# Twenty of the 120 taps of a depthwise convolution move from the vector engine to the scalar engine and accumulating DMAs

## The chip, the cores and the metric

The kernel runs on one core of one Trainium2 chip. The metric is the device time of one execution in microseconds (us), the median of several runs. Beside it stands a profiled execution of the same program; every time of a single instruction comes from that one.

## What is computed

Two transformer-like blocks in sequence on one sequence of 512 tokens and 1024 features, all in float32. The first block mixes tokens by pooling and gating, attends to a memory of 256 entries, and ends in a feed-forward part with a three-tap convolution. The second block is the one that matters here:

```
h = rms_norm(x, norm1_g)
q, k, v, glu_a, glu_b = split(h @ w_in)
q, k = rms_norm(q per head, q_norm_g), rms_norm(k per head, k_norm_g)
attn = stick_breaking_attention(q, k, v)              # 8 heads of 64, causal

c = glu_a * sigmoid(glu_b)                            # 512 tokens x 512 channels
c = causal_depthwise_conv(c, conv_dw_w, conv_dw_b)    # 31 taps
c = silu(layer_norm(c, conv_ln_g, conv_ln_b))

x = x + concat(attn, c) @ w_out
x = x + conv_ffn(rms_norm(x, norm2_g))
```

The depthwise convolution has 31 taps. For each of four chunks of 128 channels (channels lie on the partitions, the 512 tokens along the free dimension) it is 31 products of a shifted 128x512 tile with one weight per channel, added up.

## The kernel before, in words

**Products.** Float32 matrix products are done as three matmuls on operands that are split into a high and a low part (`mm3`, lines 126 to 129). Weights are loaded 1024 KB at a time into `raw` by SyncE's DMA queue, and `prep` (line 178) makes the two parts: ScalarE casts the high one (L199), and VectorE subtracts to get the low one (L205). For eight weight units of this stage (`SUMMED`, line 63) the low part is made in another way: ScalarE writes the negated weights (L202), and a DMA from GpSimd's queue adds `raw` onto that (L203, `accum_op`).

**The stage around the change.** After the first block's feed-forward part TensorE computes, in this order: the gated unit's chunks 0 and 1 (`glu`, line 697), the queries (`heads("G", ...)`), chunk 2, the keys (`heads("F", ...)`), chunk 3, the values (`project`, lines 960 to 969), and then the attention in twelve blocks (`sticks`, `breaks`, `gather`). While TensorE works on this, VectorE does the convolution's taps one at a time as filler (`conv`, L851): one instruction multiplies a shifted 128x512 view of `cc` (the slot H0) by a column of weights and adds it onto `cv` (the slot H1). One tap of each chunk is done by ScalarE, which starts the sum with the bias (L848 by way of L132). `TURNS` lists the chunk of each of the other 120 taps, and each call of `conv(n, after)` releases the next n of them, behind a given instruction.

**Heads.** For each of four tiles of 128 tokens, `heads` (line 728) multiplies into a bank of PSUM, ScalarE squares the tile (L742), VectorE sums over each head (L744), GpSimd makes the inverse root in three small instructions (L745, L746, L747: multiply and add, power, multiply), and VectorE scales the tile into `norm2` (L748, the slot D1). When all four tiles are there TensorE transposes them (L755), eight 128x128 pieces for the first two tiles and eight for the other two, and ScalarE and VectorE split the result (L143, L144) into the queries or keys that the attention reads.

**The norm.** `conv_norm` (line 884) normalizes the convolution's result over the channels. It is written behind the attention: four matmuls with ones give the mean (L889), VectorE subtracts it (L893), ScalarE squares (L895), VectorE adds up (L897), four small matmuls and a power on GpSimd give the inverse root (L902, L906, L334), one matmul spreads it (L911), VectorE scales (L915), and ScalarE applies SiLU (L917).

**Order.** The order on each engine is not the order in which the code is written. A list scheduler places each instruction at build time by its own estimate of when it can start, so a change of one part moves others; every engine then runs its list strictly in that order. Where an instruction waits, all those behind it on its engine wait too.

Of the kernel before, what the change touches and what calls it, by code (L numbers as in the profile page):

```python
# [10 lines left out]
F32 = mybir.dt.float32  # L11
F32R = mybir.dt.float32r
I32 = mybir.dt.int32
AF = mybir.ActivationFunctionType
# [65 lines left out]
def block_kernel(  # L80
# [91 lines left out]
    def half(name, a, b, dt=F32R):  # L172
        return part(slot(name, dt), a, b)
# [523 lines left out]
    def glu(i):  # L697
        pt = sta_unit(ph, pl)
        if i == 0:
            norms()  # L700
        ab = v3(t4(), 2, 512)
        dve.tensor_tensor(ab, pt, over2(rb2), ALU.mult)
        sig = act.activation(ab[:, 1, :], ab[:, 1, :], AF.Sigmoid)
        if i == 3:
            with tc.issue_after(sig.ins):
                act.preload_act_table_set(tables)
        return dve.tensor_tensor(cc[:, i, 30:542], ab[:, 0, :], ab[:, 1, :], ALU.mult)  # L707
# [67 lines left out]
    def sticks(hp, n):  # L775

        w = WIDE[n]
        zt = pair()
        z = zt[:, :, :w]

        for i, (ks, qs) in enumerate(((kT[0], qT[0]), (kT[0], qT[1]), (kT[1], qT[0]))):
            for a in STEPS[n]:
                for e in range(2):
                    hs = slice(e * HD, (e + 1) * HD)
                    pe.matmul(z[:, e, cols_of(a)], ks[hs, hp, a * P : (a + 1) * P],  # L785
                              qs[hs, hp, a * P :], start=i == 0 and a < 3, stop=False,
                              skip_group_check=True)
        for a in STEPS[n]:
            for e in range(2):
                pe.matmul(z[:, e, cols_of(a)][:, :P], identr, never, start=False, stop=False,  # L790
                          skip_group_check=True)
        ex = v3(t4(), 2, w)
        if hp < 2:
            act.activation(ex, z, AF.Abs)
        else:

            dve.tensor_scalar(ex.bitcast(I32), z.bitcast(I32), 0x7FFFFFFF, None,
                              ALU.bitwise_and)
        act.activation(ex, ex, AF.Exp, scale=-1.0)
        act.activation(ex, ex, AF.Ln, bias=1.0)  # L800
        dve.scalar_tensor_tensor(ex, z, 0.0, ex, ALU.max, ALU.add)
        zs[hp, n] = z
        return copy_split(*blk(hp, n), ex)
# [28 lines left out]

    TURNS = [0] * 8 + [0, 1] * 22 + [1, 2] * 8 + [2, 3] * 22 + [3] * 8
    done = [0] * 4
    tap = None

    def conv(n, after=None):

        nonlocal tap
        tap = after or tap
        for _ in range(min(n, len(TURNS))):
            i = TURNS.pop(0)
            k = done[i]
            done[i] += 1
            if k == 0:
                identity(cv[:, i, :], cc[:, i, 30:542], scale=par("dw_w", 4 * 30 + i),  # L848
                         bias=par("dw_b", i))
            with tc.issue_after(tap.ins) if tap else nullcontext():  # L850
                tap = dve.scalar_tensor_tensor(  # L851
                    cv[:, i, :], cc[:, i, k : k + 512], par("dw_w", 4 * k + i), cv[:, i, :],
                    ALU.mult, ALU.add)
# [2 lines left out]
    conv(8, glu(0))  # L856
    split_early(2)
    conv(16, glu(1))
    qT = heads("G", "qg", HD ** -0.5, (0, 4, 4, 8), lambda: conv(8, glu(2)), early[:2])
    kT = heads("F", "kg", 1.0, (0, 6, 5, 8), lambda: conv(12, glu(3)), early[2:])  # L860
    v2 = half("E0", 4, T, F32)
    stk = {}

    def place(i):
# [106 lines left out]
    seq = [(hp, n) for hp in range(4) for n in range(3)]  # L971

    conv(10, sticks(*seq[0]))
    conv(14, sticks(*seq[1]))
    project()
    todo = 2
    for i, x in enumerate(seq):
# [138 lines left out]
```

## Time and profile before

| | |
|---|---|
| median of 3 runs | 1245.53 us (1244.4 to 1246.41) |
| the profiled execution | 1245.94 us, its span 1244.2 us |
| TensorE busy | 1230.3 us, 99% of the span |
| VectorE busy | 754.0 us, 61% |
| ScalarE busy | 495.0 us, 40% |
| GpSimd busy | 113.5 us, 9% |

The span is the time from the first to the last instruction on the core; the rest of the 1245.94 us lies around it. PE is TensorE's matmul row, PEld its weight load, DVE VectorE, ACT ScalarE, POOL GpSimd and SP SyncE. A DMA that an engine starts is listed with that engine; the time "to landing" runs from the start of the issuing instruction to the arrival of its data.

### The profile page before, as it was taken

Reading aid. Unit: us, or ns where it says so; the run is one execution under the profiler, and the core shown is the slowest. Engines: PE = TensorE matmul, PEld = TensorE weight load, DVE = VectorE, ACT = ScalarE, POOL = GpSimd, SP = SyncE. Lnnn points to the kernel's source line nnn. Section 1 sums busy time; section 2 is a strip of 40 time slices with the busy share of each in tenths; the row PEclk is TensorE's granted clock in tenths of the full one; section 3 lists DMA queues with packets and bytes.
Section 4 is the critical chain, followed back from the end, with each engine's and each line's share of the span. In section 5 each row is a group of like instructions: output and inputs, shape, how many; then the busy total and the mean of one; then the engine's idle time right before and its main releaser. Section 6 shows DMA issues by size and latency. Waiting matters only on the chain.

```text
span 1244.2 us, 13667 instructions
## 1 busy us (share of the span) xinstructions
PE 1230.3 (99%) x5712; PEld 1014.1 (82%) x5712; DVE 754.0 (61%) x823; ACT 495.0 (40%) x534; POOL 113.5 (9%) x137
## 2 busy tenths in 40 slices
PE   9999999999999999999999999999999999999998
PEld 7889888788888888888888887667888888888887
DVE  7855634744766674466373899877575555346532
ACT  6433424623544342243255338764343333123310
POOL 1100210012000000000053440000400000000000
PEclk9999999999999999999999999899999999999999
DMA  7223222312222222222346254301322222222222
GB/s 274 101 104 132 102 102 68 136 68 98 73 100 102 102 102 102 88 85 99 119 152 169 68 130 104 106 1 68 102 102 82 89 100 102 102 102 102 84 70 83
DMA packets 21597, 126.71 MB, mean 102 GB/s; under 512 B 2336, under 2 KB 4256, under 8 KB 7840
## 3 DMA queue, kind: packets, MB, share of 16 engines
q1 hardware_dynamic: 20096, 117.20, 26.7%
q0 software_dynamic: 1152, 8.39, 3.5%
q8 instruction: 44, 0.72, 0.2%
q10 hardware_dynamic: 288, 0.26, 0.1%
q14 instruction: 17, 0.14, 0.0%
HBM read 115.35 MB, written 2.10 MB: 94 GB/s over the span
## 4 chain that ended last, share of the span: by engine, by line
PE 90%; DVE 4%; POOL 2%; ACT 2%; issue 1%; DMA 1%; SPq 0%; DVEq 0%; POOLq 0%; ACTq 0%
PE pp L129 27%; PE pp L127 27%; PE pp L128 27%; DVE H L851 2%; PE ps L128 1%; PE ps L129 1%; PE ps L127 1%; POOL col L746 1%; PE pp L814 1%; PE pp L817 1%; PE ps L829 1%; DMA wlo<-raw 1%; POOL col L745 1%; PE pp L785 0%; PE ps L326 0%
## 5 line engine op out<-in xcount | busy, mean ns | idle before, releaser
L199 ACT CAST whi<-raw 128x2048 fp32r<-128x2048 f32 (+3 forms) x109 | 197.9, 1817 | 415.5 <-PE pp L128 335.7
L129 PE MATMUL pp<-B,wlo 128*128 128x512 f32 x672 | 262.5, 391 | 0.2
L127 PE MATMUL pp<-B,whi 128*128 128x512 f32 x672 | 261.7, 390 | 0.8 <-ACT whi L199 0.7
L128 PE MATMUL pp<-C,whi 128*128 128x512 f32 x672 | 262.2, 390 | 0.0
L205 DVE TENSOR_TENSOR wlo<-raw,whi 128x2048 fp32r<-128x2048 f32 (+3 forms) x101 | 219.3, 2172 | 66.1 <-ACT whi L199 65.6
L128 PE MATMUL pp<-G,whi 128*128 128x512 f32 x448 | 175.0, 391 | 0.0
L129 PE MATMUL pp<-F,wlo 128*128 128x512 f32 x416 | 162.2, 390 | 0.0
L127 PE MATMUL pp<-F,whi 128*128 128x512 f32 x416 | 161.5, 389 | 0.0
L129 PEld LDWEIGHTS pp<-B,wlo 128*128 128x128 f32 x672 | 126.1, 188 | 28.2 <-DVE wlo L205 1.5
L127 PEld LDWEIGHTS pp<-B,whi 128*128 128x128 f32 x672 | 126.3, 188 | 28.0 <-ACT whi L199 1.7
L128 PEld LDWEIGHTS pp<-C,whi 128*128 128x128 f32 x672 | 126.2, 188 | 26.8 <-issue 0.5
L128 PEld LDWEIGHTS pp<-G,whi 128*128 128x128 f32 x448 | 84.1, 188 | 17.5 <-issue 0.2
L655 DVE SCALAR_TENSOR_TENSOR H<-H,sm,H 128x512 f32<-128x512 f32 x132 | 92.8, 746 | 0.7
L634 DVE TENSOR_TENSOR A<-pp,A 128x1024 f32<-128x1024 f32 x23 | 28.2, 1224 | 105.5 <-PE pp L129 105.5
L129 PEld LDWEIGHTS pp<-F,wlo 128*128 128x128 f32 x416 | 78.1, 188 | 16.5 <-issue 0.2
L127 PEld LDWEIGHTS pp<-F,whi 128*128 128x128 f32 x416 | 78.1, 188 | 16.4 <-issue 0.2
L851 DVE SCALAR_TENSOR_TENSOR H<-H,sm,H 128x512 f32<-128x512 f32 x120 | 83.2, 742 | 2.7 <-ACT H L132 2.5
L660 DVE TENSOR_TENSOR H<-pp,rb 128x1024 f32<-128x1024 f32 x22 | 26.8, 1224 | 50.6 <-PE pp L129 44.4
L132 ACT ACTIVATE H<-H,sm 128x512 f32<-128x512 f32 x70 | 54.3, 808 | 4.6 <-DVE H L707 4.6
L1010 DVE TENSOR_TENSOR H<-pp,rb 128x512 f32<-128x512 f32 x22 | 15.2, 691 | 60.4 <-PE pp L129 55.3
L127 PE MATMUL pp<-D,whi 128*128 128x512 f32 x112 | 43.6, 389 | 0.0
L128 PE MATMUL pp<-E,whi 128*128 128x512 f32 x112 | 43.6, 389 | 0.0
(315 smaller groups left out, 1826.3 us busy)
## 6 DMA issues: line engine op xcount, KB each, us to landing
raw<-in_wts SPq DMA_DIRECT2D x99, 1024.0 KB, 4.8
wlo<-raw POOLq DMA_DIRECT2D x8, 1024.0 KB, 7.0
raw<-in_wts SPq DMA_DIRECT2D x8, 768.0 KB, 4.2
A<-in_xT SPq DMA_DIRECT2D x3, 512.0 KB, 6.7
out<-A SPq DMA_DIRECT2D x3, 512.0 KB, 2.8
D<-in_memT SPq DMA_DIRECT2D x1, 1024.0 KB, 11.4
raw<-in_wts SPq DMA_DIRECT2D x3, 256.0 KB, 7.6
A<-in_xT SPq DMA_DIRECT2D x2, 256.0 KB, 3.9
```

The costliest lines, as they stand in the source:

```text
L127: pe.matmul(out, wh, xh, start=start, stop=False, **kw)
L128: pe.matmul(out, wh, xl, start=False, stop=False, **kw)
L129: pe.matmul(out, wl, xh, start=False, stop=stop, **kw)
L132: act.activation(out, in_, AF.Identity, scale=scale, bias=bias)
L199: act.copy(hi[:, cs], raw[:, cs])
L205: dve.tensor_tensor(lo[:, cs], raw[:, cs], hi[:, cs].bitcast(F32), ALU.subtract)
L634: dve.tensor_tensor(hu, pt, hu, ALU.add)
L655: dve.scalar_tensor_tensor(dst, hs[:, k : k + 512], w(k), dst, ALU.mult, ALU.add)
L660: dve.tensor_tensor(hs[:, :, 2:], pt, over2(rb), ALU.mult)
L745: pool.tensor_scalar(ms, ms, rr2[:, t : t + 1], EPS, ALU.mult, ALU.add)
L851: tap = dve.scalar_tensor_tensor(cv[:, i, :], cc[:, i, k : k + 512], par("dw_w", 4 * k + i), cv[:, i, :], ALU.mult, ALU.add)
L1010: dve.tensor_tensor(hs[:, 2:514], pt[:, 0, :], rb, ALU.mult)
```

## The change

Chunks 0 and 1 lose ten taps each on VectorE (k = 20 to 29). Their products are made by ScalarE (L847). The product for k = 20 is written into a tile in the slot D0 directly, one half for each chunk. Each of the nine others goes into a second tile in the same slot, and a DMA from GpSimd's queue adds it onto the first (L849, 256 KB each, 18 in all). Each of these DMAs reads and writes what the one before it for the same chunk wrote, so it waits for that one's landing; and the next product of that chunk overwrites the tile that the DMA reads, so ScalarE waits for the landing as well. Behind `heads("F", ...)` VectorE adds the two sums onto `cv` (L875, one 128x1024 instruction). The order of the remaining 100 taps is rewritten, and the second block of the attention releases 11 taps instead of 14. In the changed file `conv`'s tap is L863.

```diff
-    TURNS = [0] * 8 + [0, 1] * 22 + [1, 2] * 8 + [2, 3] * 22 + [3] * 8
+    TURNS = [0] * 8 + [0, 1] * 12 + [1] * 8 + [2] * 27 + [2, 3] * 3 + [3] * 27
     done = [0] * 4
     tap = None
+    aside = []
+
+    def by_dma():
+
+        tl = half("D0", 4, T, F32)
+        aside.append(tl[:, 0:2, :])
+        for k in range(20, 30):
+            for i in range(2):
+                out = tl[:, i, :] if k == 20 else tl[:, 2 + i, :]
+                act.activation(out, cc[:, i, k : k + 512], AF.Copy, scale=par("dw_w", 4 * k + i))
+                if k > 20:
+                    pool.dma_start(out=tl[:, i, :], in_=out, accum_op=ALU.add)
...
     conv(8, glu(0))
     split_early(2)
     conv(16, glu(1))
+    by_dma()
     qT = heads("G", "qg", HD ** -0.5, (0, 4, 4, 8), lambda: conv(8, glu(2)), early[:2])
     kT = heads("F", "kg", 1.0, (0, 6, 5, 8), lambda: conv(12, glu(3)), early[2:])
     v2 = half("E0", 4, T, F32)
+    dve.tensor_tensor(cv[:, 0:2, :], cv[:, 0:2, :], aside[0], ALU.add)
...
     conv(10, sticks(*seq[0]))
-    conv(14, sticks(*seq[1]))
+    conv(11, sticks(*seq[1]))
```

On GpSimd the keys' stretch stood so before: the weights' low part of chunk 3 has just been issued, and the inverse roots of three of the keys' four tiles follow (`col_4825`, `col_4857`, `col_4896`), then the DMA for the low part of the values' first weight unit, and then the fourth tile (`col_4933`).

```order
92 L745 TENSOR_SCALAR col_4825<-col_4825,rr_4358 128x8
93 L746 TENSOR_TENSOR col_4825<-col_4825,mhalf 128x8
94 L747 TENSOR_SCALAR col_4825<-col_4825,rr 128x8
95 L745 TENSOR_SCALAR col_4857<-col_4857,rr_4358 128x8
96 L746 TENSOR_TENSOR col_4857<-col_4857,mhalf 128x8
97 L747 TENSOR_SCALAR col_4857<-col_4857,rr 128x8
98 L745 TENSOR_SCALAR col_4896<-col_4896,rr_4358 128x8
99 L746 TENSOR_TENSOR col_4896<-col_4896,mhalf 128x8
100 L747 TENSOR_SCALAR col_4896<-col_4896,rr 128x8
101 L203 DMA wlo<-raw 128x2048
102 L745 TENSOR_SCALAR col_4933<-col_4933,rr_4358 128x8
```

In the change the same stretch, with the same tiles named `col_4865`, `col_4897` and `col_4935`, begins with four accumulations, and four more stand between the inverse roots.

```order
99 L203 DMA wlo<-raw 128x2048
100 L849 DMA D_4550<-D_4550 128x512 x4
101 L745 TENSOR_SCALAR col_4865<-col_4865,rr_4358 128x8
102 L746 TENSOR_TENSOR col_4865<-col_4865,mhalf 128x8
103 L745 TENSOR_SCALAR col_4897<-col_4897,rr_4358 128x8
104 L747 TENSOR_SCALAR col_4865<-col_4865,rr 128x8
105 L746 TENSOR_TENSOR col_4897<-col_4897,mhalf 128x8
106 L849 DMA D_4550<-D_4550 128x512 x2
107 L747 TENSOR_SCALAR col_4897<-col_4897,rr 128x8
108 L745 TENSOR_SCALAR col_4935<-col_4935,rr_4358 128x8
109 L849 DMA D_4550<-D_4550 128x512
110 L746 TENSOR_TENSOR col_4935<-col_4935,mhalf 128x8
```

Then come the last accumulation, the L747 of that tile, the DMA for the values' weights and the fourth tile (`col_4972`); the other ten accumulations stand in the same way among the queries' inverse roots, ahead of chunk 3's weight DMA.

On VectorE the end of the keys' stretch stood so before: the sum over the heads of the keys' last tile, five taps, and the scaling of that tile.

```order
354 L748 TENSOR_TENSOR D_4359<-pp,col_4896 128x512
355 L851 SCALAR_TENSOR_TENSOR H_2138<-H_2137,sm,H_2138 128x512 x3
356 L744 TENSOR_REDUCE col_4933<-D_4359 128x8
357 L851 SCALAR_TENSOR_TENSOR H_2138<-H_2137,sm,H_2138 128x512 x5
358 L748 TENSOR_TENSOR D_4359<-pp,col_4933 128x512
```

In the change the sum of the accumulated products comes in between, and fewer taps stand around it.

```order
354 L748 TENSOR_TENSOR D_4359<-pp,col_4935 128x512
355 L863 SCALAR_TENSOR_TENSOR H_2138<-H_2137,sm,H_2138 128x512
356 L744 TENSOR_REDUCE col_4972<-D_4359 128x8
357 L875 TENSOR_TENSOR H_2138<-H_2138,D_4550 128x1024
358 L863 SCALAR_TENSOR_TENSOR H_2138<-H_2137,sm,H_2138 128x512 x2
359 L748 TENSOR_TENSOR D_4359<-pp,col_4972 128x512
```

So L875 now stands ahead of the last scaling (L748) that the keys' transposes need. The end of VectorE's list in the attention stood so before, with the norm behind the last block.

```order
414 L851 SCALAR_TENSOR_TENSOR H_2138<-H_2137,sm,H_2138 128x512
415 L801 SCALAR_TENSOR_TENSOR t_5589<-pp,t_5589 128x1024
416 L136 TENSOR_TENSOR C_5242<-t_5589,C_5242 128x1024
417 L893 SCALAR_TENSOR_TENSOR H_2138<-ps_5651,H_2138 128x512 x4
418 L897 TENSOR_TENSOR t_5657<-t_5657,t_5660 128x512
```

In the change the norm's instructions (L907, L911, L920, L922 and L929 of the changed file) stand among the attention's last five blocks.

```order
400 L801 SCALAR_TENSOR_TENSOR t_5483<-pp,t_5483 128x768
401 L920 TENSOR_SCALAR col_5696<-ps_5691 128x4
402 L922 TENSOR_TENSOR t_5698<-ident,col_5699 128x512
403 L136 TENSOR_TENSOR D_5133<-t_5483,D_5133 128x768
404 L797 TENSOR_SCALAR t_5536<-pp 128x768
405 L801 SCALAR_TENSOR_TENSOR t_5499<-pp,t_5499 128x1024
406 L929 TENSOR_TENSOR H_2138<-H_2138,ps_5702 128x512 x4
```

The last tap stands ahead of all of these, and no tap is left in the last five blocks.

## Rows read from the trace of the kernel before

**Rows 1.** The page: busy time, share of the span and instructions of each engine.
```profile
PE 1230.3 (99%) x5712; PEld 1014.1 (82%) x5712; DVE 754.0 (61%) x823; ACT 495.0 (40%) x534; POOL 113.5 (9%) x137
```

**Rows 2.** Busy time by stretch: us, each engine's busy time, granted clock, DMA share, GB/s.
```profile
690.00:745.00 55.00, 55.00 (x255) 45.77 (x254) 52.06 (x78) 14.91 (x16) 27.27 (x26) 1.00 0.37 93
745.00:780.00 35.00, 34.87 (x188) 27.93 (x186) 34.97 (x49) 28.88 (x29) 2.65 (x3) 1.00 0.49 125
780.00:832.00 52.00, 46.27 (x280) 33.23 (x279) 40.62 (x50) 34.09 (x43) 0.00 (x0) 0.90 0.19 55
```

**Rows 3.** The same view, three stretches of 10 us.
```profile
780.00:790.00 10.00, 8.27 (x61) 5.29 (x60) 9.44 (x14) 8.65 (x12) 0.00 (x0) 0.96 0.95 279
790.00:800.00 10.00, 9.62 (x45) 8.43 (x46) 7.07 (x9) 5.62 (x8) 0.00 (x0) 0.52 0.01 2
850.00:860.00 10.00, 9.35 (x41) 7.39 (x41) 10.00 (x14) 6.49 (x9) 0.10 (x1) 1.00 0.30 107
```

**Rows 4.** The page: groups of instructions; count, busy us, mean ns, idle before.
```profile
L851 DVE SCALAR_TENSOR_TENSOR H<-H,sm,H 128x512 f32<-128x512 f32 x120 | 83.2, 742 | 2.7 <-ACT H L132 2.5
```

**Rows 5.** Timeline of DVE: start us, us, instruction, count.
```profile
706.39 5.38 DVE L851 SCALAR_TENSOR_TENSOR H<-H,sm,H 128x512 f32<-128x512 f32 x8
742.60 0.69 DVE L748 TENSOR_TENSOR D<-pp,col 128x512 f32<-128x512 f32 x1 [0.66 <-POOL col L747]
```

**Rows 6.** The chain that ended last, in the attention: start us, us, what.
```profile
817.17 0.66 DVE H L851
...
822.20 0.66 DVE H L851
```

**Rows 7.** Groups on POOL from 690 to 743 us.
```profile
L746 POOL TENSOR_TENSOR col<-col,mhalf 128x8 f32<-128x8 f32 x8 | 14.9, 1864 | 0.6
L745 POOL TENSOR_SCALAR col<-col,rr 128x8 f32<-128x8 f32 x8 | 6.8, 856 | 17.4 <-DVE col L744 17.2
L747 POOL TENSOR_SCALAR col<-col,rr 128x8 f32<-128x8 f32 x8 | 3.7, 460 | 0.8
```

**Rows 8.** A group on ACT from 650 to 760 us.
```profile
L143 ACT ACTIVATE B<-A,fg 128x512 fp32r<-128x512 f32 x2 | 1.3, 708 | 0.0
```

**Rows 9.** The weights' accumulating DMAs: issue and landing, 1024 KB each.
```profile
L203 POOL DMA_DIRECT2D wlo<-raw x8: 838/920/1047, 656.1 to 776.6; - x8
...
DMA to landing us min/median/max: 6.9/7.0/8.9
```

**Rows 10.** The page: the DMA queue of GpSimd; packets, MB, share of 16 engines.
```profile
q0 software_dynamic: 1152, 8.39, 3.5%
```

**Rows 11.** Timeline of POOL, four of the weights' DMAs and instructions of the keys.
```profile
686.78 0.84 POOL L203 DMA_DIRECT2D wlo<-raw  x1 [13.46 <-ACT wlo L202]
714.15 0.93 POOL L203 DMA_DIRECT2D wlo<-raw  x1 [8.40 <-ACT wlo L202]
721.90 1.27 POOL L745 TENSOR_SCALAR col<-col,rr 128x8 f32<-128x8 f32 x1 [6.82 <-DVE col L744]
735.86 0.93 POOL L203 DMA_DIRECT2D wlo<-raw  x1 [0.53 <-ACT wlo L202]
742.25 0.31 POOL L747 TENSOR_SCALAR col<-col,rr 128x8 f32<-128x8 f32 x1
772.05 0.86 POOL L203 DMA_DIRECT2D wlo<-raw  x1 [22.51 <-ACT wlo L202]
776.60 0.85 POOL L203 DMA_DIRECT2D wlo<-raw  x1 [3.69 <-ACT wlo L202]
```

**Rows 12.** Timeline of ACT: chunk 3's weights, high and low part.
```profile
710.11 1.93 ACT L199 CAST whi<-raw 128x2048 fp32r<-128x2048 f32 x1 [10.10 <-PE pp L128]
711.94 1.91 ACT L202 ACTIVATE wlo<-raw 128x2048 fp32r<-128x2048 f32 x1
```

**Rows 13.** Timeline of PE: the keys' transposes and the values' first matmul.
```profile
744.55 1.91 PE L755 MATMUL pp<-ident,D 128*128 128x128 f32 x16
746.21 0.48 PE L127 MATMUL ps<-whi,B 128*128 128x512 f32 x1
```

## The prediction

> **What bounds the kernel now.** I read the page's busy shares first: TensorE is busy for 99% of the span, the others for 61% and less [rows 1]. So a gain must come from where TensorE waits, and the windows by stretch say where that is. From 690 to 745 us (queries, gated unit, keys) it is busy all the time, and VectorE, with the taps, for 52.06 of 55 us; to 780 us TensorE misses 0.13 us; in the attention, 780 to 832 us, it misses 5.7 of 52 us at a mean granted clock of 0.90 [rows 2]. The finer windows put the low clock in one place: TensorE is busy for 8.27 of the 10 us to 790, and in the next ten the granted clock is 0.52, which is close to the lower of its two levels (1.2 of 2.4 GHz); after the attention one more gap of 0.65 us is left, at 850 to 860 [rows 3]. That is all there is to win: 5.7 us of gaps, about 5 us of clock (0.10 of 52 us), 0.65 us behind it. The taps are 120 instructions, 83.2 us of VectorE [rows 4], and nearly all of this runs beside TensorE. In the chain that ended last a tap stands between two steps of the attention only now and then; in its late part I find two, 0.66 us each [rows 6].
>
> **What is removed.** Twenty taps. One alone takes 742 ns [rows 4], but eight in a row take 5.38 us [rows 5], so one costs 0.66 us and twenty 13.2 us. VectorE gets L875 for it, a sum over 128x1024 (1.2 us by the taps' rate of about 0.6 us for 512), so it loses about 12 us. In the stretch to 745 us that is worth nothing by itself, since TensorE doesn't wait there. In the attention the last five blocks are free of taps, but the norm now stands among them, on a similar number of instructions (four, three and four of 512 columns). I count as a gain the two taps in the chain (1.3 us) and the gap behind the attention (0.65 us), which the earlier norm should close: 2 us.
>
> **What is added on ScalarE.** Twenty activations of 128x512. No row shows this form; the nearest, with a column as scale and both sides in SBUF, takes 708 ns [rows 8]. That is 14 us, in a stretch where ScalarE is busy for 14.91 of 55 us [rows 2]: there is room. Not free is their place: all but the first few wait for a DMA's landing, and ScalarE's own list waits behind them.
>
> **What is added on GpSimd.** Eighteen DMA issues. The issuing instruction takes 0.92 us for 1024 KB [rows 9]; I take the same, since the number of rows is the same (128): 16.6 us. GpSimd was busy for 27.27 of the 55 us [rows 2], so 44 are taken by work alone, and it has to wait in order too.
>
> **The price of one accumulation** (256 KB) is nowhere in the trace. The nearest rows are the weights' accumulations, 1024 KB in 7.0 us from issue to landing [rows 9]. That queue's packets took 3.5% of 16 engines over 1244.2 us [rows 10], 43.5 us for eight DMAs or 5.4 us each; the other 1.6 us are fixed. With a quarter of the bytes I estimate 1.6 + 1.35 = 3.0 us. The lower bound is 1.6 us (bytes cost nothing), the upper one 7.0 us (all of it is fixed); I take 3.0, because the share of the packets is measured.
>
> The Trainium skill (DMA: Bandwidth & Descriptors, Anatomy of one DMA) gives about 2.0 us plus the bytes at 436 GB/s for a DMA from this queue, by which 256 KB would take an estimated 2.6 us, and 1024 KB 4.4 us where the row has 7.0. By that price each round would be 0.4 us shorter and the stall below about 3 us.
>
> **A round** of one chunk is the product (0.7 us), the hand-over to GpSimd (0.3 us: ScalarE's L202 ends at 713.85 us [rows 12] and L203 starts at 714.15 [rows 11]), and the landing (3.0 us): 4.0 us. Nine rounds are 36 us. From 690 us, when chunk 1 is there, that would end at 726 and do no harm. What makes it worse is the order, in two ways.
>
> First, the weights' DMAs use the same queue. Of two that were issued 4.55 us apart, at 772.05 and 776.60 us [rows 11], one must be the longest of the eight, 8.9 us instead of 7.0 [rows 9]; I read it as the second one waiting for the first one's bytes. So an accumulation issued behind one of them lands about 1.35 us after it. This happens twice: behind the DMA of 686.78 us (landing 693.8, so the first accumulation lands at about 695) and behind chunk 3's.
>
> Second, all three lists are strict. Following them by hand: the rounds up to k = 25 end in products at about 713.4 us, because GpSimd now does the issues between the queries' inverse roots and each waits for the other. ScalarE's cast and negation for chunk 3's weights stand behind that product: 713.4 + 1.8 + 1.9 [rows 12] = 717.1 instead of 713.85, so L203 goes at 717.4 and lands at 724.4. The accumulations for k = 26 stand behind it in the queue and land at 725.8 and 727.1. Only then can ScalarE make the two products for k = 27 (726.5 and 727.8), and only when GpSimd has issued both (729.0) does its list reach the L745 of the keys' first tile, which it did at 721.90 before [rows 11]: 7.1 us late. From there GpSimd has no pause: four tiles of 0.86 + 1.86 + 0.46 us [rows 7] are 12.7 us, five DMA issues 4.7 us, and some 2 us of hand-overs and two waits, together 19.4 us. The keys' last L747 ends at 748.4 us, against 742.56 before [rows 11].
>
> **What that costs.** VectorE scales the last tile in 0.69 us [rows 5] and is done at about 749.2. TensorE's transposes stand at 744.55 us, 16 of them in 1.91 us; the second half would begin at 745.4 [rows 13] and now waits for 749.2: 3.8 us. Behind it in TensorE's list are the values. Their first low part is issued at about 743 instead of 735.86 [rows 11] and lands at about 750, needed at 746.3 [rows 13] plus the stall, so it adds nothing. Then VectorE, with five taps, the gated unit's product, four taps, the two splits of the keys and a tap behind L748, ends the splits at about 759.5; TensorE wants the low part after the transposes' rest (0.9 us), 26 matmuls of the values (5.9 us) and two thirds of the first score block (2.2 us), at 758.3: 1.2 us more. L875 itself waits for the last accumulation (issued at about 742, landing at 745) and is done well before L748 may start; at 4.5 us a landing it would be the later of the two. Sum: 3.8 + 1.2 - 2.0 = +3.0 us, on a profiled execution of 1245.94 us, which lies 0.4 us above the median: 1249 us.
>
> **Rivals.** (a) The clock falls. A stall of 4 us is longer than any pause of TensorE in these rows, and after the 1.7 us missed in the ten to 790 us the granted clock was 0.52 for ten [rows 3]. A second such spell, now with the dense matmuls of the values under it, costs another 5 us: 1254 us. For it speaks the size of the stall, against it that TensorE is dense on both sides of it, which it wasn't at 785. The Trainium skill (TensorE: Matmul & The Clock Gate, Part 1: The HAM clock gate) says the same: the clock falls to half when the engine has been idle for a while and returns after sustained work. [...]
>
> (b) The accumulations cost what the large ones do, 7.0 us. A round is then 8.0 us, nine are 72, and the last product lands at 690 + 72 = 762; L747 follows at about 766, and TensorE stalls for some 21 us: about 1265 us. Against it speaks that the packets' time is most of the 7.0 us.
>
> (c) It is faster. If GpSimd keeps the keys' last L747 within about 744 us (two thirds of the waits above gone, say landings near 1.6 us), the second half of the transposes doesn't wait, and VectorE enters the attention with 12 us less to do. Then the 2 us above are won, and up to 5 more if the low clock at 790 us doesn't come: 1239 to 1243 us. For it: VectorE is busy for 40.62 of 52 us there [rows 2]. Against it: the chain's late part shows only two taps in its way [rows 6], and the norm fills the place of the others. The point that decides is L747's end at 744 us.
>
> (d) No change: a stall of 1 to 3 us and the gain of 2 us cancel; 1244 to 1248 us.
>
> **How the numbers follow.** I count 0.2% (2.5 us) as what a measurement of this kernel can tell. Forecast, a stall of 4 to 7 us less the gain, 1248 to 1252 us: 0.42. (a) 0.20. (b) or anything near it, over 1257 us: 0.08. (c) 0.14. (d) 0.16, and a part of the forecast's low end lies within 0.2% as well (0.04). That gives faster 0.14, same 0.20, slower 0.66. The range reaches from part of (c) to (a) and the start of (b): 1242 to 1257 us, which leaves out about 2 in 10. The forecast's own range is 1248 to 1252.
>
> **What would show it.** Right: L849 lands about 3.0 us after its issue, and near 8 us for the two behind chunk 3's weights; the keys' last L747 ends near 748 us; TensorE waits some 4 us for L748 ahead of the second eight transposes; ScalarE's cast for chunk 3 starts near 713 us, not 710. Wrong: TensorE without a gap up to 750 us means that GpSimd had more room than I gave it, and the sign may turn. A clock at half behind 750 us is (a); L849 above 4.5 us leads to (b). If the attention takes clearly fewer than the 52 us of before, I have taken the taps' part in it too low.

## The result and the profile after

The changed kernel takes 1259.93 us (median of four runs, 1259.23 to 1260.54), the kernel before beside it 1245.34 us: a ratio of 1.0119, 95% interval 1.0103 to 1.0135. It is 14.6 us slower; forecast were 3.5 us. The profiled execution has a span of 1257.5 us against 1244.2, so 13.3 us are to be found in it. One execution of the run e10 below took 1734.7 us; its figures are those of its other three. The page's row for the engines, which answers to [rows 1]:

```profile
PE 1233.4 (98%) x5712; PEld 1015.7 (81%) x5712; DVE 745.6 (59%) x804; ACT 508.0 (40%) x554; POOL 127.4 (10%) x155
```

The edit did what it says: ScalarE has 20 instructions more, GpSimd 18 more, VectorE 19 fewer and 8.4 us less work, where about 12 were forecast. Yet no busy share says where 13 us went. Three marks in TensorE's timeline do: the start of the first score matmul (L785), the start of the last group of matmuls of the attention with the values (L829), and the end. From the first copy of the stage's norm factors (L347, 679.02 us before, 678.87 after) to the first scores it was 73.3 us and is now 84.4; from there to the last L829 it was 88.45 and is 86.4; behind it 403.45 and now 407.8. So 11.1 us are lost **ahead of** the attention, 2.0 won **in** it, 4.3 lost **behind** it. The windows around the losses, to be read against [rows 2, 3] (us, each engine's busy time, granted clock, DMA share, GB/s):

```profile
740.00:750.00 10.00, 7.58 (x37) 5.93 (x35) 8.49 (x14) 6.60 (x7) 7.72 (x10) 1.00 0.68 118
750.00:760.00 10.00, 5.38 (x20) 4.71 (x21) 8.63 (x11) 5.28 (x5) 4.50 (x4) 0.66 0.93 184
850.00:860.00 10.00, 8.63 (x37) 6.16 (x34) 5.58 (x6) 8.38 (x11) 0.00 (x0) 1.00 0.00 0
860.00:870.00 10.00, 7.45 (x26) 5.64 (x25) 8.20 (x11) 0.00 (x0) 0.10 (x1) 0.83 0.18 63
```

In the first two TensorE, which had hardly a gap there before [rows 2], is idle for 7 of 20 us, and the granted clock of the second is 0.66, with matmuls at the lower of the two levels in it. Its timeline names what it waits for (in brackets the idle time ahead and its releaser; it answers to [rows 13]):

```profile
748.65 1.06 PE L755 MATMUL pp<-ident,D 128*128 128x128 f32 x8 [2.13 <-DVE D L748]
754.62 1.94 PE L755 MATMUL pp<-ident,D 128*128 128x128 f32 x8 [4.91 <-DVE D L748]
756.21 0.78 PE L127 MATMUL ps<-whi,B 128*128 128x512 f32 x1
756.78 0.63 PE L128 MATMUL ps<-wlo,B 128*128 128x512 f32 x1
757.21 0.63 PE L129 MATMUL ps<-whi,C 128*128 128x512 f32 x1
...
758.87 0.40 PE L128 MATMUL ps<-wlo,B 128*128 128x512 f32 x1
759.11 0.39 PE L129 MATMUL ps<-whi,C 128*128 128x512 f32 x1
```

The keys' transposes wait 7.0 us for the scaled tiles, the queries' 1.5 us more (two waits, 0.64 and 0.88 us). Behind the stall the first five steps from one matmul to the next take 0.36 to 0.57 us, then 0.23: that is 1.0 us more than the same five steps took before. The last eight transposes, 1.94 us where sixteen had taken 1.91, cost another 1.0. That makes 10.5 of the 11.1 us. VectorE waits for GpSimd's L747 there, and GpSimd's timeline answers to [rows 11]:

```profile
694.20 0.88 POOL L849 DMA_DIRECT2D D<-D  x1
696.53 0.86 POOL L849 DMA_DIRECT2D D<-D  x1 [1.46 <-ACT D L847]
...
721.64 0.85 POOL L203 DMA_DIRECT2D wlo<-raw  x1 [2.75 <-ACT wlo L202]
722.25 1.13 POOL L849 DMA_DIRECT2D D<-D  x1
...
731.16 0.86 POOL L849 DMA_DIRECT2D D<-D  x1 [5.93 <-ACT D L847]
...
733.76 1.35 POOL L745 TENSOR_SCALAR col<-col,rr 128x8 f32<-128x8 f32 x1
...
753.43 0.31 POOL L747 TENSOR_SCALAR col<-col,rr 128x8 f32<-128x8 f32 x1
```

The keys' first L745 starts at 733.76 us, before it was 721.90. Ahead of it GpSimd waits 5.93 us for a product, and that product waits for a landing, as ScalarE's timeline shows (its chunk-3 cast answers to [rows 12]):

```profile
701.42 0.73 ACT L847 ACTIVATE D<-H,sm 128x512 f32<-128x512 f32 x1 [4.70 <-DMA D<-D]
702.69 0.72 ACT L847 ACTIVATE D<-H,sm 128x512 f32<-128x512 f32 x1 [0.55 <-DMA D<-D]
...
717.64 1.89 ACT L199 CAST whi<-raw 128x2048 fp32r<-128x2048 f32 x1
...
730.14 0.72 ACT L847 ACTIVATE D<-H,sm 128x512 f32<-128x512 f32 x1 [3.75 <-DMA D<-D]
```

All instructions of the line L849 together (duration in ns min/median/max; who waited for it: us, times; landing in us):

```profile
L849 POOL DMA_DIRECT2D D<-D x18: 847/894/1281, 688.6 to 746.5; - x18
...
  ACT D L847: 32.1, 14
...
DMA to landing us min/median/max: 3.3/3.6/7.8
```

Behind the attention the cause is another. ScalarE's timeline there:

```profile
849.69 1.28 ACT L1000 ACT_TABLE_LOAD   x1
850.99 2.93 ACT L931 ACTIVATE H<-H,sm 128x512 f32<-128x512 f32 x4
853.82 0.56 ACT L135 CAST G<-ps 128x512 fp32r<-128x512 f32 x1
```

L135 casts the attention's last output, for which the output product waits. Before, it stood right behind that output, 0.04 us behind the last L829's end, and the norm's SiLUs came later:

```profile
841.87 0.59 ACT L135 CAST G<-ps 128x512 fp32r<-128x512 f32 x1 [2.68 <-PE ps L829]
```

Now the norm is done early, inside the attention, so its table load and four SiLUs are ready and stand ahead of the cast. TensorE then waits twice:

```profile
854.44 0.96 PE L127 MATMUL pp<-G,whi 128*128 128x512 f32 x3 [1.37 <-ACT G L135]
863.42 0.50 PE L127 MATMUL pp<-G,whi 128*128 128x512 f32 x1 [2.55 <-DVE A L971]
```

The second wait goes back to the same cast: VectorE's next L136 waits for it, and L971 comes behind that. Together the two are 3.3 us more than the 0.65 us of before; behind the second the granted clock is 0.83 over ten us, with matmuls 0.43 us apart.

### The profile page after: what moved, and what is told of

Read it like the earlier page. It is cut to its first block, busy times and chain, and to the rows that moved or that the text cites. A ratio compares the mean times of both kernels' runs of the same rounds, so it can differ in the third digit from the quotient of the medians.

```text
span 1257.5 us, 13714 instructions
## 1 busy us (share of the span) xinstructions
PE 1233.4 (98%) x5712; PEld 1015.7 (81%) x5712; DVE 745.6 (59%) x804; ACT 508.0 (40%) x554; POOL 127.4 (10%) x155
## 4 chain that ended last, share of the span: by engine, by line
PE 89%; DVE 3%; ACT 2%; DMA 2%; POOL 2%; issue 1%; SPq 0%; DVEq 0%; ACTq 0%; POOLq 0%
PE pp L129 27%; PE pp L127 27%; PE pp L128 27%; DMA D<-D 2%; PE ps L128 1%; PE ps L129 1%; PE ps L127 1%; POOL col L746 1%; DVE H L863 1%; PE pp L814 1%; PE ps L829 1%; PE pp L817 1%; PE pp L785 1%; PE ps L326 0%; DMA A<-in_xT 0%
## 5 line engine op out<-in xcount | busy, mean ns | idle before, releaser
L655 DVE SCALAR_TENSOR_TENSOR H<-H,sm,H 128x512 f32<-128x512 f32 x132 | 92.8, 748 | 0.7
L129 PEld LDWEIGHTS pp<-F,wlo 128*128 128x128 f32 x416 | 78.2, 188 | 16.4 <-issue 0.2
L863 DVE SCALAR_TENSOR_TENSOR H<-H,sm,H 128x512 f32<-128x512 f32 x100 | 72.5, 748 | 3.9 <-ACT H L132 2.5
L129 PE MATMUL pp<-D,wlo 128*128 128x512 f32 x112 | 43.6, 390 | 0.0
```

The source lines that it names most:

```text
L129: pe.matmul(out, wl, xh, start=False, stop=stop, **kw)
L655: dve.scalar_tensor_tensor(dst, hs[:, k : k + 512], w(k), dst, ALU.mult, ALU.add)
L863: tap = dve.scalar_tensor_tensor(cv[:, i, :], cc[:, i, k : k + 512], par("dw_w", 4 * k + i), cv[:, i, :], ALU.mult, ALU.add)
```

## The experiments

All runs in one table. "Ahead" runs from L347's first copy to the first score matmul, "in" from there to the last matmul with the values, "behind" to the end of the span; all three are of the profiled execution, in us. Every ratio is against the kernel before on the same chip. The profiled execution is one of several: e2's took 1248.1 us where the median is 1251.3, and those of e3, e17 and e18 2.0 to 2.4 us more than theirs, so a line's parts need not add up to its median. In the stretch ahead two kernels with the same lists on GpSimd and ScalarE there still differ by 0.8 us (changed and e5) and 1.2 us (e4 and e18).

| kernel | median us | ratio (95%) | ahead | in | behind |
|---|---|---|---|---|---|
| before | 1245.3 | 1 | 73.3 | 88.5 | 403.5 |
| changed | 1259.9 | 1.0119 (1.0103 to 1.0135) | 84.4 | 86.4 | 407.8 |
| e1 no replacement | 1250.2 | 1.0039 (1.0024 to 1.0054) | 73.3 | 90.9 | 406.2 |
| e2 products only | 1251.3 | 1.0055 (1.0038 to 1.0071) | 73.3 | 88.0 | 406.2 |
| e3 weights on VectorE | 1260.9 | 1.0124 (1.0102 to 1.0146) | 85.7 | 90.7 | 406.2 |
| e4 half | 1253.0 | 1.0061 (1.0046 to 1.0076) | 77.4 | 88.0 | 407.8 |
| e5 SiLUs behind the cast | 1254.4 | 1.0075 (1.0060 to 1.0090) | 85.3 | 86.5 | 401.7 |
| e6 as e1 and e5 | 1245.6 | 1.0002 (0.9993 to 1.0012) | 73.3 | 90.8 | 401.7 |
| e7 late | 1263.3 | 1.0147 (1.0132 to 1.0162) | 73.3 | 104.8 | 405.4 |
| e8 as e7 and e5 | 1261.3 | 1.0134 (1.0119 to 1.0149) | 73.3 | 101.8 | 405.4 |
| e9 interleaved | 1259.4 | 1.0121 (1.0106 to 1.0136) | 82.5 | 90.0 | 406.2 |
| e10 as e9 and e5 | 1256.2 | 1.0096 (1.0076 to 1.0116) | 81.3 | 91.5 | 401.7 |
| e11 as e1, norm held | 1245.5 | 1.0002 (0.9993 to 1.0011) | 73.3 | 85.8 | 405.4 |
| e12 as e9, norm held | 1255.7 | 1.0086 (1.0067 to 1.0105) | 82.5 | 86.6 | 403.4 |
| e13 three pairs | 1259.7 | 1.0119 (1.0104 to 1.0134) | 86.6 | 86.5 | 407.8 |
| e14 as e13, e9 and e5 | 1253.2 | 1.0068 (1.0052 to 1.0085) | 82.3 | 88.6 | 401.8 |
| e15 as e13, e9, norm held | 1252.4 | 1.0060 (1.0045 to 1.0075) | 81.2 | 84.7 | 405.3 |
| e16 half, among queries, e5 | 1248.4 | 1.0021 (1.0012 to 1.0030) | 73.6 | 91.4 | 401.6 |
| e17 as e16, norm held for e5 | 1249.6 | 1.0032 (1.0020 to 1.0043) | 73.6 | 91.5 | 403.3 |
| e18 as e4 and e5 | 1248.9 | 1.0031 (1.0019 to 1.0043) | 76.2 | 91.3 | 401.6 |

The theory at the start: accumulations in GpSimd's list cost the 11 us, the order of the norm the rest. The rivals: ScalarE's products and their places, the weights' transfers, or a cost of the new order alone.

### e1 and e2: the parts by themselves

```diff
-    by_dma()
-    dve.tensor_tensor(cv[:, 0:2, :], cv[:, 0:2, :], aside[0], ALU.add)
```

> Twenty taps of chunks 0 and 1 are left out altogether: no products on ScalarE, no accumulating DMAs, no addition of their sum. VectorE loses the same 12 us as in the changed kernel, and nothing takes their place. Theory (the accumulations in GpSimd's list cost about 11 us ahead of the attention, and the rewritten order about 2 us behind it): the stretch up to the first scores returns to that of before, the span is that of before plus 0 to 3 us, 1245 to 1248 us. Rival (the stall hid a gain): 1233 to 1242 us, since 12 us less VectorE work then shorten the attention. Rival (the new order of taps and norm is what costs): 1252 to 1258 us.

For e2 only the DMAs go:

```diff
-                if k > 20:
-                    pool.dma_start(out=tl[:, i, :], in_=out, accum_op=ALU.add)
```

> The twenty products stay on ScalarE, the eighteen accumulating DMAs are left out, so what VectorE adds is one product instead of the sum of ten. Theory (GpSimd's list): the DMAs behind which the inverse roots and the weights' transfers stood are gone, so the stretch ahead of the attention grows only by what ScalarE's 14 us of products delay, 1 to 3 us; 1246 to 1250 us. Rival (ScalarE's products ahead of the cast of chunk 3's weights cost, not the transfers): 1255 to 1260 us.

The stretch ahead takes 73.3 us in both, as before to 0.1 us. So the accumulations cause the whole 11.1 us, and the products, 14 us of ScalarE's work, cost nothing there. But e1 is also 4.8 us *slower* than before, with 9 us less work on VectorE and nothing added, outside what the theory allowed: 2.5 us in the attention and 2.7 behind it. The new order costs by itself; e6 and e11 below take this apart.

### e3: the weights' low parts without GpSimd

```diff
-SUMMED = [i for i, p in enumerate(PLAN) if p[0] == "w_in_2"][1:]
+SUMMED = [i for i, p in enumerate(PLAN) if p[0] == "w_in_2"][1:3]
```

> The changed kernel, but the low parts of three weight chunks whose transfers stand in GpSimd's list among the accumulations are subtracted on VectorE, as other chunks' are. Theory A (the weights' transfers, 1 MB each behind the accumulations on one queue, are what the matmuls wait for): most of the 11 us come back, 1249 to 1253 us. Theory B (the inverse roots of the keys stand behind the accumulations in the list, whatever the weights do): 1 to 3 us come back, 1256 to 1259 us. That VectorE's three more subtractions cost more than this: 1260 to 1263 us.

L203 now runs four times instead of eight. Nothing comes back: 85.7 us ahead. VectorE's subtraction comes late in its turn; of what TensorE waits for ahead of the attention, the first row is new:

```profile
PE ps L128 <- DVE wlo L205: 3.4, 1, 3.4
PE pp L755 <- DVE D L748: 2.8, 1, 2.8
```

The keys' last L747 ends at 752.8 us instead of 753.7: GpSimd waits 2.1 us for VectorE's sum ahead of this root, where it waited 1.2, and the root's L745 takes 4.6 us instead of 1.3. So the run puts other waits in place of those it removes, and does not settle what share the weights' transfers had.

### e4: half of the taps

```diff
-        for k in range(20, 30):
+        for k in range(25, 30):
```

The ten taps that go back to VectorE are put into `TURNS`, and the attention's second block releases 21 taps instead of 11.

> Only taps 25 to 29 of the two chunks go by way of ScalarE and the accumulations (8 DMAs instead of 18), the other ten are back on VectorE. Theory (each round of product and accumulation is 4 to 5 us of GpSimd's list): five rounds fewer end the list some 20 us earlier, before the roots of the keys are due, so nearly nothing is left of the 11 us: 1245 to 1250 us. Rival (each accumulation costs the same wherever it ends): 8/18 of 14.5 us, 1251 to 1253 us. Rival (a fixed cost of the rewritten order): 1257 to 1260 us.

8 accumulations cost 4.1 us ahead, 18 cost 11.1: 0.5 and 0.6 us each, near the rival's proportion, and not nothing as the theory had it. They already stall the queries' transposes.

### e5 and e6: the SiLUs behind the last cast

The table load and the SiLUs are put behind the cast of the last output in ScalarE's list (`cast` is that instruction):

```diff
-    with tc.issue_after(weighted.ins):
+    with tc.issue_after(cast.ins):
         act.preload_act_table_set("silu_and_others")
...
-            with tc.issue_after(weighted.ins):
+            with tc.issue_after(cast.ins):
                 act.activation(ci, ci, AF.Silu, scale=par("ln_g", i), bias=par("ln_b", i))
```

> The changed kernel, but ScalarE's table load for the norm's four SiLUs, and these four, stand behind the cast of the last pair's attention output instead of ahead of it. Theory (the 4.3 us that are lost behind the attention are this cast, which waited for 1.3 us of table load and 2.9 us of SiLU): the cast starts some 3 us earlier, TensorE's gaps of 1.4 and 2.6 us behind the attention close, and 2 to 4 us come back: 1256 to 1258 us. Rival (the loss behind the attention is VectorE's, which has 4.6 us of products with the residual there, whatever the cast does): 1259 to 1261 us.

> Twenty taps of chunks 0 and 1 are left out, with nothing in their place, and the SiLUs stand behind the last cast. Theory (the loss of 4.8 us without any replacement was half the cast behind the attention, half the attention itself): 1246.5 to 1248.5 us. If VectorE's 12 us were worth what they are long, as a rival would have it, 1235 to 1242 us; if the place of the SiLUs is nothing, 1250 us.

5.5 us come back in e5, more than expected: behind the attention it takes 401.7 us, 6.1 less than the changed kernel and 1.8 less than the kernel before, since the early norm is then a gain. ScalarE's timeline of e5:

```profile
851.85 0.59 ACT L834 CAST G<-ps 128x512 fp32r<-128x512 f32 x1 [1.18 <-PE ps L831]
852.45 1.28 ACT L1004 ACT_TABLE_LOAD   x1
853.75 2.94 ACT L935 ACTIVATE H<-H,sm 128x512 f32<-128x512 f32 x4
```

All six runs with an early norm and this order have 401.6 to 401.8 us there. And e6 is the change without its costs: no taps, nothing in their place, no late cast. It is no faster than the kernel before, and 1 us faster than the theory had it.

### e7 and e8: the same accumulations during the attention

The products are held behind the exponentials of the attention's blocks, one k for each of ten blocks; the tiles are others, and the sum is added ahead of the norm:

```diff
         weighted = breaks(*x)
+        if i < 10:
+            by_dma(20 + i)
```

> The same twenty products and eighteen accumulations, each pair held behind one of ScalarE's exponentials of the attention, where GpSimd's list holds nothing else; the sum is added just ahead of the norm. Theory (the 11 us ahead of the attention are the roots and the weights' transfers behind the accumulations): the first scores start as before, at 752 us, and the span is before plus what 14 us of products cost ScalarE in the attention and what the norm loses: 1245 to 1251 us. Rival (accumulations cost wherever they stand, by traffic on the queues): 1256 to 1260 us.

> As the run before it, and the SiLUs stand behind the last cast. If both theories hold, 1243 to 1248 us, the best of these kernels; if the norm, now late, has no SiLU ahead of the cast, the same as the run before it within 1 us.

Ahead all is as before, 73.3 us, which is the theory once more. But both times lie over 10 us above the theory's ranges, and that of e7 above the rival's too: in e7 the attention takes 104.8 us, 16.4 more than before. TensorE's busy time is 8.3 us of these, at a mean granted clock of 0.85 where it was 0.94; the rest is waiting. ScalarE has 14 us of products more among the attention's steps, and 6.4 us of waits for landings, with the attention's own steps behind them, as here (e7):

```profile
818.56 0.72 ACT L847 ACTIVATE acc<-H,sm 128x512 f32<-128x512 f32 x1 [2.60 <-DMA t<-acc]
819.19 0.57 ACT L135 CAST G<-ps 128x512 fp32r<-128x512 f32 x1
```

Behind the attention e8 takes what e7 takes, 405.4 us: with the norm late, the place of the SiLUs makes no difference there. The 2 us between the two runs are in the attention.

### e9 and e10: accumulations behind the roots, none ahead

One pair for each of the eight tiles of queries and keys, its DMAs behind that tile's root in GpSimd's list, its products behind that tile's square on ScalarE:

```diff
-            pool.tensor_scalar(ms, ms, rr[:, t : t + 1], None, ALU.mult)
+            root = pool.tensor_scalar(ms, ms, rr[:, t : t + 1], None, ALU.mult)
+            by_dma((22 if name == "G" else 26) + t, square, root)
```

> The same products and the same eighteen accumulations on the same queue, but dealt out: one pair behind each of the eight tiles' inverse roots in GpSimd's list, with its products behind that tile's squares on ScalarE, so that no root stands behind a transfer that has still to land. Theory (it is the order, roots behind waits for landings): the first scores start at 752 to 756 us instead of 763, and 7 to 11 us come back, 1249 to 1253 us. Rival (the traffic itself, 18 accumulations beside the weights' loads on the DMA engines): 1257 to 1260 us.

> As the run before it, with the SiLUs behind the last cast. If the two causes are separate and add, 5.5 us less than that run: 1243 to 1248 us, about the kernel before; faster than before by 2 us or more only if the lighter VectorE shortens the attention, which the run without any replacement did not show.

The theory in its simple form falls: 82.5 us ahead, 1.9 less than the changed kernel, and a time in the rival's range. The keys' last L747 is 5 us earlier and the transposes wait 3.8 us instead of 8.6, but the wait has moved on. ScalarE's products still wait 31.8 us for landings, the longest time with the squares of a tile behind it:

```profile
734.55 0.72 ACT L850 ACTIVATE D<-H,sm 128x512 f32<-128x512 f32 x1 [7.87 <-DMA D<-D]
...
736.51 0.58 ACT L742 ACTIVATE D<-pp 128x512 f32<-128x512 f32 x1
```

GpSimd issues the values' weights (L203) at 744.51 us instead of 735.86, and TensorE now waits for these, again with matmuls at half pace behind it:

```profile
749.68 1.06 PE L756 MATMUL pp<-ident,D 128*128 128x128 f32 x8 [2.09 <-DVE D L749]
...
752.81 0.79 PE L128 MATMUL ps<-wlo,B 128*128 128x512 f32 x1 [1.82 <-DMA wlo<-raw]
753.40 0.63 PE L129 MATMUL ps<-whi,C 128*128 128x512 f32 x1
```

In e10 the place of the SiLUs gives 4.5 us behind the attention, but the attention itself takes 1.4 us more than in e9, and the time is some 8 us above what was expected.

### e11 and e12: the norm held

```diff
+            with tc.issue_after(last.ins):
                 dve.scalar_tensor_tensor(ci, mu, -1.0 / 512.0, ci, ALU.mult, ALU.add)
```

> Twenty taps are left out with nothing in their place, and the norm's first VectorE operations stand behind the last scores' split, so that the norm ends where it ended before. If the norm inside the attention ate what the lighter VectorE gives, 1238 to 1243 us. If the attention is a chain of three engines in which VectorE's taps fill waits, 1244 to 1248 us, whatever the norm does.

> The accumulations dealt out among the roots, the norm held as in the run before it. By the first theory 1240 to 1245 us, the best of all; by the second 1245 to 1250 us, the same as the interleaved kernel with the SiLUs behind the cast.

With no replacement the attention takes 85.8 us, 2.6 less than before, and what follows 1.9 more: the norm's last matmul stands at 851.06 us, where it stood at 844.62. Again there is no gain in sum. The median of e12 is 3.7 us below that of e9; in the profiled executions the attention and what follows are both shorter. With 82.5 us ahead it stays over 5 us above both of its forecasts.

### e13 to e15: three pairs of tiles for the products

```diff
-                out = tl[:, i, :] if k == 20 else tl[:, 2 + i, :]
+                out = tl[:, i, :] if k == 20 else pairs[k % 3][i]
```

> The changed kernel with three pairs of tiles for the products in turn instead of one, so that a product waits for the landing of the accumulation three rounds before it. If the landings that ScalarE and GpSimd wait for are the cause, its waits for them fall from 32 us to under 10 us, the first scores start at 753 to 757 us instead of 763, and the time is 1250 to 1255 us. If it is GpSimd's issuing and the traffic, 1258 to 1261 us.

> Three pairs of product tiles, the accumulations dealt out behind the roots, the SiLUs behind the last cast. If landings are the cause, nothing is left of the 11 us: 1244 to 1249 us, about the kernel before. If it is issuing and traffic, as with one pair, 1255 to 1258 us.

> Three pairs of product tiles, the accumulations dealt out, and the norm held behind the last scores' split. If landings are the cause, 1243 to 1248 us; if it is issuing and traffic, 1254 to 1257 us.

e13 takes the time of the changed kernel, as the rival had it, with 2 us more ahead. ScalarE waits half as long for landings (16.0 us by its rows, 32.1 in the changed kernel; under 10 were expected), but now GpSimd itself does, because each accumulation reads what the last one wrote (what its idle time ahead of L851 ended with: us, times):

```profile
  DMA D<-D: 8.8, 4
  ACT D L742: 6.2, 1
  DMA D<-t: 6.1, 4
  DMA D<-acc: 3.2, 3
```

With both, in e14, GpSimd waits for VectorE ahead of the keys' first root, and from there to the last root it works without a pause. One tile takes 3.65 us for the root and 1.84 for two issues, of the 5.9 us between tiles, and the values' weights wait their turn:

```profile
726.04 1.28 POOL L745 TENSOR_SCALAR col<-col,rr 128x8 f32<-128x8 f32 x1 [7.66 <-DVE col L744]
...
737.93 1.28 POOL L745 TENSOR_SCALAR col<-col,rr 128x8 f32<-128x8 f32 x1
739.29 2.06 POOL L746 TENSOR_TENSOR col<-col,mhalf 128x8 f32<-128x8 f32 x1
741.45 0.31 POOL L747 TENSOR_SCALAR col<-col,rr 128x8 f32<-128x8 f32 x1
741.91 1.84 POOL L858 DMA_DIRECT2D D<-t  x2 [0.15 <-issue]
743.08 1.55 POOL L203 DMA_DIRECT2D wlo<-raw  x1
```

That issue is 7.2 us later than before [rows 11], TensorE waits 1.99 us for it and 3.2 for the transposes, and 82.3 us ahead are left. GpSimd's own time is not all of this: the keys' last L747 is 5.4 us later than before, and 4.1 us of that are there at the first root (721.90 us in [rows 11]), which waits for VectorE's sum, after the queries' transposes had waited 2.2 us for their tiles. The times of e14 and e15 lie between the two forecasts, 1.6 us and more below the range of issuing and traffic and 4 us above that of landings.

### e16 to e18: eight accumulations, where there is room

Ten taps aside, a pair of accumulations behind each of the queries' roots and none among the keys', three pairs of product tiles:

```diff
+            if name == "G":
+                by_dma(26 + t, square, root)
```

> Ten taps (25 to 29 of two chunks) go aside, with eight accumulations, one pair behind each of the queries' four roots and none among the keys'; three pairs of product tiles; the SiLUs behind the last cast. If the named causes are the whole cause, the first scores start at 752.5 to 755 us, and the shorter attention and the earlier norm give back 2 to 4 us: 1241 to 1246 us, faster than the kernel before or the same. If the accumulations cost wherever they stand, 1248 to 1251 us.

> The same, with the norm held behind the last scores' split in place of the SiLUs behind the cast. 1242 to 1246 us if the causes are the named ones; 1248 to 1251 us if not.

> The run with half of the taps, one pair of product tiles and the scheduler's own order, with the SiLUs behind the last cast: its 1253.0 us less what that place gave in the changed kernel, 5.5 us: 1246.5 to 1249 us, with the first scores at 756 us as there.

For eight accumulations this settles the stretch ahead: 73.6 us in e16 and e17, 0.3 more than before, with TensorE's transposes whole as in [rows 13] and the first scores of e16 at 752.46 us, as forecast:

```profile
744.43 1.91 PE L757 MATMUL pp<-ident,D 128*128 128x128 f32 x16
```

The same eight accumulations in the scheduler's places and with one pair of tiles cost 2.9 us there (e18, as forecast; 4.1 in e4). Which of the two, the place or the tiles, does it was not tried apart, nor all eighteen in such places. And the expected gain doesn't come: behind the attention e16 wins 1.8 us, and in it loses 3.0. So the times of e16 and e17 fall into the ranges of the rival (that accumulations cost wherever they stand), though not for its reason. No run beats the kernel before.

## Why the prediction was wrong

The direction was right, the size was not: +14.6 us where +3.5 was forecast, above the range. Of the profiled execution's 13.3 us the sum had 3.0. Ahead of the attention it had 3.8, and 11.1 were measured; in it 1.2 of loss less 1.3 of gain, and a gain of 2.0 was measured; behind it a gain of 0.65, and a loss of 4.3 was measured. Two steps failed: the price of the accumulations, and what the earlier norm does behind the attention. Step by step:

**The structure of the stall was right.** ScalarE's cast for chunk 3, GpSimd's L203, the keys' first L745, the last L747, the transposes waiting for L748: each was named, and each is late in that order. From the keys' first L745 to the last L747's end 19.4 us were forecast and 20.0 measured (733.76 to 753.74).

**The price of an accumulation was too low, and this is the step that failed ahead of the attention.** I took 3.0 us, 1.6 fixed and 1.35 for the bytes. The bytes were about right: GpSimd's queue, by the page's row, took 5.7% of 16 engines over 1257.5 us, 71.7 us, against 43.5 [rows 10], so an estimated 1.57 us for each of 18 if the weights' eight took what they took before. By that the fixed part is 2.0 us, since the median landing is 3.6.

```profile
q0 software_dynamic: 3744, 13.11, 5.7%
```

The Trainium skill's figure (DMA: Bandwidth & Descriptors, Anatomy of one DMA), from which I had estimated 2.6 us, is further off. And a median is not the price of a chain in series: the slowest ones set it. The pair issued at 694.20 and 696.53 us released its products at 701.42 and 702.69, 7.2 and 6.2 us later, in ten microseconds with a DMA share of 0.95, where 0.63 was before. From 690 to 704 us one load of 1024 KB (`raw`) ran on SyncE's queue, q1, beside three of the accumulations:

```profile
q1 hardware_dynamic: 144, 1.05, 24.3%
raw<-in_wts SPq DMA_DIRECT2D x1, 1024.0 KB, 6.4
D<-D POOLq DMA_DIRECT2D x3, 256.0 KB, 6.1
```

Its packets took 3.4 of these 14 us, about what the pair landed later than the median (3.6 and 2.6 us), and the load itself landed after 6.4 us instead of 4.7. I counted collisions with the weights' accumulations alone (near 8 us for the two behind chunk 3's: 7.8 is the maximum), not with such loads. That the load is the reason is a reading of these rows. The pair's first landing is 4.2 us above the 3.0; the cast for chunk 3 came at 717.64 us instead of the forecast 713.4, 4.2 us late as well, and everything behind it was 4 to 5 us later than worked out.

**What that made of the stall.** The last eight transposes were forecast for 749.2 us and started at 754.62, which is 5.4 of the 7.3 us that were missing ahead. That the queries' transposes wait too (1.5 us), and the keys' first eight (2.1 us), I had not seen, but it does not come on top: L748 sets the start of the last eight whatever TensorE waited for before. The rest is rival (a), which came with the stall: 2.0 us of slow matmuls and transposes, not 5. The Trainium skill's rule (TensorE: Matmul & The Clock Gate, Part 1: The HAM clock gate), that the clock halves after idling and returns under sustained work, agrees with these rows. The further 1.2 us for the keys' splits shrank to one wait of 0.6 us (L785 for L144), just behind the first scores.

**The gain of 2 us is the other step that failed.** The part in the attention, 2.0 us measured against 1.3, was met by luck: in e1 and e6, with the same taps gone and the same order, the attention takes 2.5 and 2.3 us longer than before. The other part had the wrong sign. I wrote that the earlier norm should close the gap of 0.65 us behind the attention; it opened one, because the SiLUs it had ready went ahead of the cast (+4.3 us, shown by e5: with them behind it, 1.8 us of gain). I had costed an earlier step without asking what it would then stand in front of.

**That the taps are not what bounds the attention held.** e6 and e11 take away 20 taps for nothing and are 1.0002 of the kernel before. In all runs but e7 and e8 the attention takes 84.7 to 91.5 us, without relation to VectorE's work in it: 88.0 us at 75.9 us of VectorE (e4), 90.8 at 67.6 (e6), 86.4 at 68.3 (the changed kernel). That the order in which three engines hand over sets it is my reading, not shown; the mean granted clock there differs too (0.94 before, 0.96 in the changed kernel and e6, 1.00 in e4 and e15). Which hand-overs make e16 5 us longer there than e5 is not settled.

**The cause of the 11 us** is the accumulations: without them, and with the products left in, the stretch takes 73.3 us (e2). How they cost it is, as far as it was tried, three limits one behind another: landings in series through one pair of product tiles (e9 leaves ScalarE's wait), landings in series through the one sum (e13 moves that wait to GpSimd), and GpSimd's own time among the keys, with the values' weights next in its list (e14). The third is read from e14's timeline alone, where 4.1 us of the delay stand ahead of the keys' first root. Lifting the first two left 8 to 9 us (e14, e15). With eight accumulations, none among the keys and three pairs of tiles, 0.3 us is left (e16), but that is also fewer than half of them; no run has eighteen ahead of the attention without the loss. No run moves or removes the load that stands beside the slow landings.

## What to carry to other kernels

In this kernel a chain of accumulating DMAs cost its slowest landings, one after another, on each list that waited for it. For such a chain, sum up the waits of the engine that makes the data and of the one that issues, and ask what is next in both lists. Work that is taken off a filler engine is worth only what the trace shows it holding up; run it once with the work simply missing before building the replacement. When a step becomes ready earlier, look at what it will overtake on its own engine, above all ahead of the one instruction that the matmuls wait for.

## What was not expected of the hardware

Accumulations of a quarter of the bytes landed in half the time at the median, 3.6 us for 256 KB against 7.0 for 1024 KB, where 3.0 was forecast; the slowest took 7.8, behind a weights' accumulation on the same queue. GpSimd's issue costs the same for both sizes, 0.89 and 0.92 us at the median; this was as forecast.
